# Strassen's seven products in an encoder block's gate and up projections, with the activations kept in DRAM and the merge's weights loaded once

## The chip, the cores and the metric

The kernel runs on one core of a Trainium2 chip. The metric is the device time of one execution in microseconds (us), the median of several runs. The engines are TensorE (PE in the profile; PEld is its weight load), VectorE (DVE), ScalarE (ACT), GpSimd (POOL) and SyncE (SP), whose queue issues every DMA of this kernel. SBUF is the memory on the chip, with 128 partitions; PSUM holds the results of matmuls; DRAM is the memory behind the DMAs.

## The reference

One encoder block over 1024 tokens and 16 learned ones ahead of them, in float32, width 1024. A mixer (retention and an attention with low-rank projections, merged by gates) and then a SwiGLU network of hidden width 2816:

```python
y_ret = (silu(rg) * y_ret) @ w_ret_out
y_mla = _mla_attention(q_nope, q_rope, k_nope, k_rope, v).reshape(B, L, 512) @ w_mla_out
merged = sigmoid(a_gret) * y_ret + sigmoid(a_gmla) * y_mla
h = h + merged @ w_o
u = _rmsnorm(h, norm_ffn_w)
h = h + (silu(u @ w_gate) * (u @ w_up)) @ w_down
return _rmsnorm(h, norm_final_w)[:, 16:]
```

## The kernel before

Everything is kept transposed: features on the partitions, the 1024 tokens along the free dimension, in two halves (c = 0, 1) of 512. A matrix product keeps float32 accuracy by splitting both operands x into a high part in the matmul's type (`hi`, a cast on ACT) and the rest (`lo = x - hi`, a subtraction on DVE). Each product of 128 features is then three matmuls, high by high, high by low and low by high (`mm3`, L117 to L119). Weights come from DRAM by `weights` (L109 the load, L112 the cast, L113 the low part), each as a block of 128 output features.

The order of the instructions on each engine is set by the Tile framework's scheduler, which works ahead as far as the buffers of a pool go. A tile's pool and its count of buffers so decide how early its load or split can stand.

The change lies in the last third of the program:

- Attention, 8 heads by 4 query chunks (`units`). It writes its output to DRAM (`o_d`) for the first six heads and to SBUF (`o3`) for the last two. The gates' and retention's results lie in DRAM as `s_d` and `r_d`.
- Load of `o_d` and its split (L803, L804) at the end of attention.
- Merge: for c, for m (8 blocks of 128 features): w_mo's block, four products of 128 features, times `s_d` (DVE, L825), plus `r_d` (POOL, L826), and a split (L812, L813). The block's weights are loaded for each c, 16 loads.
- w_o: for c, for m: weights, eight products of 128 features, plus x (L855) gives the residual `h2`, which stays in SBUF; times the norm's weights and split (ACT L857, DVE L858) into `u2`; squares on ACT, summed on POOL (L865, `ssum`). At the end of each c the norm's factor per token (`rs2_b`, L838 to L148).
- Gate and up: the 22 blocks of 128 hidden features are worked in groups of 6, 6, 6 and 4 (`FG`). For each block and each c, gate and up take 24 matmuls each; then `rs2_b` times gate (L891), Silu on ACT (L892), `rs2_b` times up (L893), their product on POOL (L894), and its split (L896, L897) into `hid`.
- Down: after each group, for 8 blocks m, the group's share of the down projection is added to `h2` (L919). In the last group the second half of the tokens is done in two chunks of 256, and the last norm and the stores (`finish`, L872, L875) follow.

```python
def gemm_s(ps, w, xs, kt, c, cols=slice(0, 512)):
    wh, wl = w
    for k in range(kt):
        ks = slice(k * P, (k + 1) * P)
        xh, xl = xs[k][c]
        mm3(ps, wh[:, ks], wl[:, ks], xh[:, cols], xl[:, cols], k == 0, k == kt - 1)
```

Of the kernel before, what the change touches and what calls it, by code (L numbers as in the profile page):

```python
# [35 lines left out]
FG = ((0, 6), (6, 6), (12, 6), (18, 4))  # L36

# [5 lines left out]
def build(nc, tc, A, out):  # L43
# [57 lines left out]
    l_d = mk(dram, (H, NB, P), "l_d")  # L101

# [18 lines left out]
    def gemm(ps, w, xs, kt, lo, n):  # L121
        wh, wl = w
        for k in range(kt):
            ks = slice(k * P, (k + 1) * P)
            xh, xl = xs[k]
            mm3(ps, wh[:, ks], wl[:, ks], xh[:, lo : lo + n], xl[:, lo : lo + n], k == 0, k == kt - 1)

# [446 lines left out]
    with ExitStack() as c1:  # L574
# [100 lines left out]
        def mix_values(hh, qc, pt, lb):  # L675
# [11 lines left out]
            if hh < H - 2:  # L687
                pool.tensor_mul(ta, ta, lb)
                store(o_d[hh // 2, hs, c], ta)
            else:  # L690
                pool.tensor_mul(o3[hs, c], ta, lb)
# [34 lines left out]
        wnext, late = None, None  # L726
# [6 lines left out]
        for i, (hh, qc) in enumerate(units):  # L733
# [3 lines left out]
            if hh % 2 == 1 and p < 3:  # L737
# [7 lines left out]
                elif qc == 2:  # L745
                    heads_q(p + 1, wnext[0], *QCH[1])
                    heads_q(p + 1, wnext[0], *QCH[2])
                    if p == 2:
                        right.close()
                        wp3 = sb(right2, "w3", 3, side="right")  # L750
                        wr3 = sb(right2, "w3r", 2, side="right")
                        t3 = sb(right2, "t3", 2, side="right")
                        t3b = sb(right2, "t3b", 3, side="right")
                        o3p = sb(right2, "o3", 1, side="right")
                        o3 = mk(o3p, (P, S), "o3")
# [14 lines left out]
    with ExitStack() as c1:  # L770
        wp = wp3
        hp = sb(c1, "h2")
        h2 = mk(hp, (P, KT, S), "h2")
        pm = sb(c1, "ps_mm3", 6, space=PSUM)
        pr_ = sb(c1, "ps_r3", 2, space=PSUM)
        r2c = mk(hp, (P, 32), "r2c")[:, :NB]
        rs2_b = mk(hp, (P, S), "rs2_b")
        slot_a = sb(c1, "slot_a", 16)
        slot = sb(c1, "slot", 40)
        ssum = [mk(hp, (P, 512), f"ssum{c}") for c in range(2)]  # L780

        def slots(pl=None):
            return mk(pl or slot, (P, 512), "slot", F32R), mk(pl or slot, (P, 512), "slot", F32R)

        def gemm_s(ps, w, xs, kt, c, cols=slice(0, 512)):
            wh, wl = w
            for k in range(kt):
                ks = slice(k * P, (k + 1) * P)
# [3 lines left out]
        o = []  # L792
        for k in range(4):
            oc = []
            for c in range(2):
                cs = slice(c * 512, c * 512 + 512)
                if k < 3:
                    raw = mk(t3, (P, 512), "ta3")
                    load(raw, o_d[k, :, cs])
                else:  # L800
                    raw = o3[:, cs]
                oh, ol = slots(slot_a)
                act.copy(oh, raw)  # L803
                dve.tensor_sub(ol, raw, f(oh))  # L804
                oc.append((oh, ol))
            o.append(oc)
        mg = [[None, None] for _ in range(KT)]
        held = None

        def split_merged(m, c, r):  # L810
            gh, gl = slots()
            act.copy(gh, r)  # L812
            dve.tensor_sub(gl, r, f(gh))  # L813
            mg[m][c] = (gh, gl)

        for c in range(2):
            cs = slice(c * 512, c * 512 + 512)
            for m in range(KT):
                w = weights(wp, A["w_mo"][m], 512, "w", wr3)
                sg, r = mk(t3b, (P, 512), "tb3"), mk(t3b, (P, 512), "tc3")  # L820
# [3 lines left out]
                gemm_s(ps, w, o, 4, c)  # L824
                dve.tensor_mul(sg, ps, sg)  # L825
                pool.tensor_add(r, r, sg)  # L826
                if held:
                    split_merged(*held)
                held = (m, c, r)
        split_merged(*held)  # L830
# [15 lines left out]
        u2 = [[None, None] for _ in range(KT)]  # L846
        for c in range(2):
            for m in range(KT):
                w = weights(wp, A["w_o"][m], D, "w", wr3)
                xk = mk(t3, (P, 512), "ta3")  # L850
                load(xk, A["xT"][m, :, c * 512 : c * 512 + 512])
                ps = mk(pm, (P, 512), "mm")
                gemm_s(ps, w, mg, KT, c)
# [152 lines left out]
```

## Time and profile before

| | |
|---|---|
| median of 3 runs | 1885.93 us (1884.98 to 1886.2) |
| profiled execution | 1885.32 us, span 1883.3 us |
| mean granted TensorE clock | 0.996 |
| TensorE busy | 1857.2 us, 99% |
| DVE, ACT, POOL busy | 880.3, 686.9, 351.4 us |
| DMA | 131.43 MB, 70 GB/s |
| merge begins | 1010.5 us |
| w_o, second half ends | about 1152 us |
| last matmul of the down projection | 1870.85 us |

A row of groups gives a line, engine, operation, tiles (out<-in), shapes, the count, the busy time, the mean of one in ns, and the idle time of the engine before them with what ended it. The chain is the sequence of work that ended last, followed back from the last instruction. In a timeline the first number is the start, the second the length, and the bracket tells how long the engine had been idle. A matmul's shown length (0.39 us) is longer than its share, since matmuls are pipelined; the distance from one to the next is what counts.

### The profile page before, as it was taken

The numbers are of one execution on the slowest core, as the hardware profiler recorded it, in microseconds if no ns is written. First come the engines' busy times: TensorE is split into PE (matmuls) and PEld (weight loads), VectorE is DVE, ScalarE is ACT, GpSimd is POOL, SyncE is SP. The second block draws the span as 40 slices with busy tenths as digits, with TensorE's granted clock in tenths as the row PEclk, the third lists the DMA queues.
The fourth block names the chain that finished last, engine by engine and source line by source line (L and its number), as shares of the span: only waits on it lengthen the run. The fifth ranks groups of instructions, "written<-read, shape, count | busy, mean of one in ns | idle before, by whom it ended". The sixth has DMA issues, their size and how long they took to land.

```text
span 1883.3 us, 24884 instructions
## 1 busy us (share of the span) xinstructions
PE 1857.2 (99%) x9806; PEld 1593.2 (85%) x9806; DVE 880.3 (47%) x1764; ACT 686.9 (36%) x1212; POOL 351.4 (19%) x324
## 2 busy tenths in 40 slices
PE   8999999999999999999999999999999999999997
PEld 8898989888888988999897788888888888888887
DVE  6654545452222436888787743223232223322335
ACT  6723233334111335877785443211122112211225
POOL 5303021204000012433423322110011001110111
PEclk9999999999999999999999999999999999999999
DMA  6101111124221213111213742111111111112112
GB/s 209 45 35 57 45 46 51 51 90 157 89 68 60 74 30 129 34 39 29 72 42 130 228 141 83 46 37 54 50 52 48 42 56 45 44 49 65 39 40 90
DMA packets 56197, 131.43 MB, mean 70 GB/s; under 512 B 7744, under 2 KB 16512, under 8 KB 56080
## 3 DMA queue, kind: packets, MB, share of 16 engines
q1 hardware_dynamic: 56080, 129.84, 21.7%
q8 instruction: 77, 1.26, 0.3%
q14 instruction: 40, 0.33, 0.1%
HBM read 108.87 MB, written 20.88 MB: 69 GB/s over the span
## 4 chain that ended last, share of the span: by engine, by line
PE 92%; DVE 3%; ACT 2%; DMA 2%; issue 1%; SPq 0%; POOL 0%; DVEq 0%; ACTq 0%; POOLq 0%
PE mm L117 24%; PE mm L119 24%; PE mm L118 24%; PE o L679 3%; PE t L649 3%; PE s L117 1%; PE s L119 1%; PE s L118 1%; PE tr L374 1%; DMA wr<-in_w_mo 1%; PE y L381 1%; PE u L362 1%; PE y L380 1%; DVE wl L113 1%; PE tr L395 1%
## 5 line engine op out<-in xcount | busy, mean ns | idle before, releaser
L119 PE MATMUL mm<-slot,wl 128*128 128x512 f32 (+1 forms) x1220 | 473.1, 388 | 0.6 <-DVE wl L113 0.5
L117 PE MATMUL mm<-slot,wh 128*128 128x512 f32 (+1 forms) x1220 | 471.6, 387 | 0.7 <-ACT wh L112 0.7
L118 PE MATMUL mm<-slot,wh 128*128 128x512 f32 (+1 forms) x1220 | 471.6, 387 | 0.0
L112 ACT CAST wh<-wr 128x1024 fp32r<-128x1024 f32 (+2 forms) x154 | 148.3, 965 | 514.6 <-PE mm L118 415.9
L119 PEld LDWEIGHTS mm<-slot,wl 128*128 128x128 f32 x1220 | 229.1, 188 | 50.6 <-DVE wl L113 4.6
L117 PEld LDWEIGHTS mm<-slot,wh 128*128 128x128 f32 x1220 | 229.1, 188 | 47.6 <-ACT wh L112 1.1
L118 PEld LDWEIGHTS mm<-slot,wh 128*128 128x128 f32 x1220 | 229.1, 188 | 46.8
L117 PE MATMUL mm<-uh,wh 128*128 128x512 f32 (+2 forms) x640 | 242.7, 379 | 1.0 <-DVE rk L317 0.6
L118 PE MATMUL mm<-ul,wh 128*128 128x512 f32 (+2 forms) x640 | 243.5, 380 | 0.0
L119 PE MATMUL mm<-uh,wl 128*128 128x512 f32 (+2 forms) x640 | 242.3, 379 | 0.0
L113 DVE TENSOR_TENSOR wl<-wr,wh 128x1024 fp32r<-128x1024 f32 (+2 forms) x154 | 189.1, 1230 | 37.2 <-ACT wh L112 35.3
L894 POOL TENSOR_TENSOR tb<-tb,ta 128x512 f32<-128x512 f32 x44 | 71.8, 1631 | 603.2 <-DVE tb L893 478.5
L117 PEld LDWEIGHTS mm<-uh,wh 128*128 128x128 f32 x640 | 120.3, 188 | 23.7 <-DVE rk L317 1.0
L119 PEld LDWEIGHTS mm<-uh,wl 128*128 128x128 f32 x640 | 120.5, 188 | 21.0
L118 PEld LDWEIGHTS mm<-ul,wh 128*128 128x128 f32 x640 | 120.2, 188 | 20.8
L893 DVE TENSOR_TENSOR tb<-mm,rs_b 128x512 f32<-128x512 f32 x44 | 30.4, 692 | 174.2 <-PE mm L119 174.1
L919 DVE TENSOR_TENSOR h<-mm,h 128x512 f32<-128x512 f32 (+1 forms) x72 | 45.2, 630 | 133.8 <-PE mm L119 133.7
L639 DVE TENSOR_SCALAR_CACHE_REDUCE pr<-s,sq_c 128x384 f32<-128x384 f32 (+1 forms) x192 | 103.0, 574 | 8.4 <-PE t L657 5.6
L652 DVE TENSOR_TENSOR ptl<-t,pth 128x512 fp32r<-128x512 f32 x128 | 85.8, 685 | 19.5 <-ACT pth L651 18.8
L896 ACT CAST slot<-tb 128x512 fp32r<-128x512 f32 x44 | 27.3, 621 | 180.3 <-POOL tb L894 180.3
L651 ACT CAST pth<-t 128x512 fp32r<-128x512 f32 x128 | 71.7, 580 | 26.6 <-PE t L649 26.2
L641 ACT ACTIVATE pr<-pr,nm 128x1040 f32<-128x1040 f32 x64 | 74.5, 1165 | 10.7 <-DVE nm L640 10.0
(324 smaller groups left out, 2993.9 us busy)
## 6 DMA issues: line engine op xcount, KB each, us to landing
wr<-in_w_in SPq DMA_DIRECT2D x37, 512.0 KB
wr<-in_w_g SPq DMA_DIRECT2D x22, 512.0 KB
wr<-in_w_u SPq DMA_DIRECT2D x22, 512.0 KB
wr<-in_w_d SPq DMA_DIRECT2D x24, 384.0 KB
wr<-in_w_o SPq DMA_DIRECT2D x16, 512.0 KB
z_d<-ay SPq DMA_DIRECT2D x16, 256.0 KB
s_d<-g SPq DMA_DIRECT2D x16, 256.0 KB
wr<-in_w_ro SPq DMA_DIRECT2D x8, 512.0 KB
```

Of the source, the lines that this page charges most:

```text
L112: act.copy(hi, raw)
L113: dve.tensor_sub(lo, raw, f(hi))
L117: pe.matmul(ps, sh, mh, start=start, stop=False)
L118: pe.matmul(ps, sh, ml, start=False, stop=False)
L119: pe.matmul(ps, sl, mh, start=False, stop=stop)
L639: dve.tensor_scalar(pr[:, c], ps[:, :n], sq_c[:, qb : qb + 1], None, ALU.mult, ALU.max, accum_out=mx[:, j : j + 1])
L641: act.activation(pr, pr, AF.Exp, bias=nm, accum_out=sums[:, s : s + 1])
L649: pe.transpose(tp[:, i, :], pr[:, b * P : (b + 1) * P], ident)
L651: act.copy(pt[0][d], tp)
L652: dve.tensor_sub(pt[1][d], tp, f(pt[0])[d])
L679: pe.matmul(po[:, :256], vt[:, b, hh, :], pt[j][:, b, :], start=(b == 0 and j == 0), stop=False)
L894: pool.tensor_mul(tu, tu, tg)
```

## The change

It does five things.

1. Gate and up are computed for blocks of 256 hidden features (11 of them) with Strassen's algorithm in Winograd's form on 2 x 2 blocks: the weights' four quarters are 256 x 256 pieces of (input half, output half), where an input half is every other block m of 128; the operand's four quarters are (input half, token half). `seven` loads four weight quarters, builds four sums of them on POOL (L905 to L908), makes seven products (`prod`, L923, 12 matmuls each, of which two add into a bank that holds an earlier product), and combines them with five additions on ACT and DVE (L933 to L942).
2. The operand's sums (`tb7`: "11", "21", "n1", "t2", "t3", "22", "t4") are made in w_o's second half from `hm` and `h0`, seven pairs of high and low tiles for each of four pairs of m. In the first gate seven (`late`) the first four products are done for three of the four pairs of m first, and then for the last pair.
3. The gated activations go to DRAM (`f_d`, L963) and come back for the down projection (L984), which stands after all 11 blocks; the residual goes to DRAM as `h_d` (L867) and is added in the first down group.
4. The merge runs over m outside and c inside, so w_mo's blocks are loaded and split 8 times in place of 16. The s_d and r_d tiles come from a pool `hr` of ten tiles that lies where the attention's memory was. All weights behind the merge come in pieces of 512 columns (`pieces`).
5. The `o_d` loads and their splits stand in attention units (6, 1) to (7, 2). The last stores leave one block at a time.

```diff
+O_AT = ((6, 1), (6, 2), (6, 3), (7, 0), (7, 1), (7, 2))
...
+    h_d = mk(dram, (KT, 2, P, 512), "h_d")
+    f_d = mk(dram, (22, 2, P, 512), "f_d")
...
+    def split(t, ph, plo):
+        hi, lo = slot(ph, F32R), slot(plo, F32R)
+        act.copy(hi, t)
+        dve.tensor_sub(lo, t, f(hi))
+        return hi, lo
...
+                        wr3 = sb(right2, "w3r", 5, side="right")
+                        wh3 = sb(right2, "w3h", 4, side="right")
+                        wl3 = sb(right2, "w3l", 4, side="right")
+                        xr = sb(right2, "x3", 14, side="right")
...
+            if (hh, qc) in O_AT:
+                g = O_AT.index((hh, qc))
+                raw = slot(wr3)
+                load(raw, o_d[g // 2, :, (g % 2) * 512 : (g % 2) * 512 + 512])
+                o_s.append(split(raw, xr, xr))
...
+        bt = sb(c1, "blocks", 58)
+        hr = sb(c1, "h3", 10)
+        ws3 = sb(c1, "w3s", 4)
+        pm = sb(c1, "ps_mm3", 7, space=PSUM)
...
-        for c in range(2):
-            cs = slice(c * 512, c * 512 + 512)
-            for m in range(KT):
-                w = weights(wp, A["w_mo"][m], 512, "w", wr3)
+        for m in range(KT):
+            w = pieces(A["w_mo"][m], 512)
+            for c in range(2):
...
-                hm = h2[:, m, c * 512 : c * 512 + 512]
+                hm = slot(hr)
                 dve.tensor_add(hm, ps, xk)
+                store(h_d[m, c], hm)
+                wc = column(C_FFN + m)
+                t7 = tb7[m // 2]
+                if c == 0:
+                    h0[m] = hm
+                    hi, lw = slot(bt, F32R), slot(bt, F32R)
+                    act.mul(hi, hm, wc)
+                    dve.scalar_tensor_tensor(lw, hm, wc, f(hi), ALU.mult, ALU.subtract)
+                    t7["11" if m % 2 == 0 else "21"] = (hi, lw)
+                elif m % 2 == 0:
+                    g12, n1 = slot(xr), slot(xr)
+                    act.mul(g12, hm, wc)
+                    dve.scalar_tensor_tensor(n1, h0[m], wc, g12, ALU.mult, ALU.subtract)
+                    t7["n1"] = split(n1, bt, bt)
+                else:
+                    g22, t2 = slot(xr), slot(xr)
+                    act.mul(g22, hm, wc)
+                    dve.tensor_add(t2, g22, n1)
+                    t7["t2"] = split(t2, bt, bt)
+                    pool.tensor_sub(g12, g22, g12)
+                    t7["t3"] = split(g12, bt, bt)
+                    t7["22"] = split(g22, bt, bt)
+                    dve.scalar_tensor_tensor(t2, h0[m], wc, t2, ALU.mult, ALU.subtract)
+                    t7["t4"] = split(t2, bt, bt)
...
+        def seven(src, pl, post, late=False):
+            a11, a21, a22, a12 = [slot(wr3) for _ in range(4)]
+            for i, t in enumerate((a11, a21, a22, a12)):
+                load(t, src[i])
+            s1, s2, s3, s4 = [slot(ws3) for _ in range(4)]
+            pool.tensor_add(s1, a21, a22)
+            pool.tensor_sub(s2, s1, a11)
+            pool.tensor_sub(s3, a11, a21)
+            pool.tensor_sub(s4, s2, a12)
...
+            todo = (("a", a11, "11"), ("b", s2, "t2"), ("c", s3, "t3"), ("d", s1, "n1"))
+            if late:
+                for t in todo:
+                    prod(*t, range(3))
+            tail = range(3, 4) if late else range(4)
+            e, v = slot(pl), slot(pl)
+            act.copy(e, prod(*todo[0], tail))
+            dve.tensor_add(e, prod(*todo[1], tail), e)
+            dve.tensor_add(v, prod(*todo[2], tail), e)
+            dve.tensor_sub(v, v, prod(*todo[3], tail))
+            post("22", v)
+            post("11", prod("a", a12, "21"))
+            t = slot(pl)
+            dve.tensor_add(t, prod("c", a22, "t4"), e)
+            post("21", t)
+            dve.tensor_sub(e, e, prod("d", s4, "22"))
+            post("12", e)
...
+            def gate_post(name, t):
+                cs = slice(0, 512) if name[1] == "1" else slice(512, 1024)
+                if name == "11":
+                    g = slot(xr)
+                    dve.tensor_mul(g, t, rs2_b[:, cs])
+                else:
+                    g = t
+                    pool.tensor_mul(g, g, rs2_b[:, cs])
+                act.activation(g, g, AF.Silu)
+                pool.tensor_mul(g, g, rs2_b[:, cs])
+                sil[name] = g
+            def up_post(name, t):
+                g = sil[name]
+                dve.tensor_mul(g, t, g)
+                store(f_d[2 * j + int(name[0]) - 1, int(name[1]) - 1], g)
...
+                    raw = slot(xr)
+                    load(raw, f_d[j, c])
+                    hc.append(split(raw, bt, bt))
...
+                if gi == 0:
+                    raw = slot(hr)
+                    load(raw, h_d[m, c])
+                    acc[m][c] = slot(bt)
+                    dve.tensor_add(acc[m][c], ps, raw)
+                    continue
```

How rows move on three engines is shown next. Tiles of the new code are all called slot; L138 is the low part of `split`, L809 that of `pieces`.

DVE in the middle of the merge, before: three rows to a step, the weight's low part (L113), the product with s_d (L825), and the low part of the merged tile (L813).

```order
L113 TENSOR_TENSOR wl_10370<-wr_10367,wh_10369 128x512
L825 TENSOR_TENSOR tb_1868_10315<-mm_10319,tb_1868_10315 128x512
L813 TENSOR_TENSOR slot_10335<-tc_1861_10287,slot_10334 128x512
L113 TENSOR_TENSOR wl_10399<-wr_10396,wh_10398 128x512
L825 TENSOR_TENSOR tb_1876_10344<-mm_10348,tb_1876_10344 128x512
L813 TENSOR_TENSOR slot_10364<-tc_1869_10316,slot_10363 128x512
```

DVE in the same place, now:

```order
L809 TENSOR_TENSOR slot_10429<-slot_10426,slot_10428 128x512
L138 TENSOR_TENSOR slot_10244<-slot_10196,slot_10243 128x512
L138 TENSOR_TENSOR slot_10267<-slot_10225,slot_10266 128x512
L834 TENSOR_TENSOR slot_10276<-mm_10280,slot_10276 128x512
L138 TENSOR_TENSOR slot_10296<-slot_10248,slot_10295 128x512
L834 TENSOR_TENSOR slot_10299<-mm_10303,slot_10299 128x512
```

The weight's low part stands once for two steps.

DVE at the end of w_o's second half, before: for each m the residual (L855), a weight's low part (L113) and the operand's low part (L858).

```order
L855 TENSOR_TENSOR h_1800_10107<-mm_11223,ta_2070_11221 128x512
L113 TENSOR_TENSOR wl_11319<-wr_11316,wh_11318 128x1024
L858 SCALAR_TENSOR_TENSOR slot_11250<-h_1800_10107,cols_74,slot_11249 128x512
L855 TENSOR_TENSOR h_1800_10107<-mm_11264,ta_2078_11262 128x512
L113 TENSOR_TENSOR wl_11445<-wr_11442,wh_11444 128x1024
L858 SCALAR_TENSOR_TENSOR slot_11291<-h_1800_10107,cols_74,slot_11290 128x512
```

DVE in the same place, now, from the last residual (L866) on: t2 (L884) and its low part, t4 (L889), the low parts of t3, "22" and t4, and between them those of two weight pieces for the first gate seven (slot_11539 and slot_11573 as high parts).

```order
L866 TENSOR_TENSOR slot_11439<-mm_11414,slot_11412 128x512
L138 TENSOR_TENSOR slot_11540<-slot_11488,slot_11539 128x512
L884 TENSOR_TENSOR slot_11443<-slot_11442,slot_11390 128x512
L138 TENSOR_TENSOR slot_11447<-slot_11443,slot_11446 128x512
L889 SCALAR_TENSOR_TENSOR slot_11443<-slot_10966,cols_74,slot_11443 128x512
L138 TENSOR_TENSOR slot_11452<-slot_11389,slot_11451 128x512
L138 TENSOR_TENSOR slot_11456<-slot_11442,slot_11455 128x512
L138 TENSOR_TENSOR slot_11461<-slot_11443,slot_11460 128x512
L138 TENSOR_TENSOR slot_11574<-slot_11483,slot_11573 128x512
L934 TENSOR_TENSOR slot_11552<-mm_11510,slot_11552 128x512
```

Where one low part followed the last residual, five operand rows and two weight rows do, ahead of the first sum of products (L934).

POOL from the end of w_o on, before: the last sums of squares and then one product for each hidden tile.

```order
L865 TENSOR_TENSOR ssum_1804_10123<-ssum_1804_10123,tc_2074_11253 128x512
L865 TENSOR_TENSOR ssum_1804_10123<-ssum_1804_10123,tc_2082_11294 128x512
L894 TENSOR_TENSOR tb_2094_11373<-tb_2094_11373,ta_2093_11372 128x512
L894 TENSOR_TENSOR tb_2100_11433<-tb_2100_11433,ta_2099_11432 128x512
L894 TENSOR_TENSOR tb_2112_11505<-tb_2112_11505,ta_2111_11504 128x512
```

POOL in the same place, now:

```order
L906 TENSOR_TENSOR slot_11643<-slot_11642,slot_11634 128x512
L907 TENSOR_TENSOR slot_11644<-slot_11634,slot_11635 128x512
L886 TENSOR_TENSOR slot_11389<-slot_11442,slot_11389 128x512
L896 TENSOR_TENSOR ssum_1824_10146<-ssum_1824_10146,slot_11464 128x512
L908 TENSOR_TENSOR slot_11645<-slot_11643,slot_11637 128x512
L905 TENSOR_TENSOR slot_11791<-slot_11784,slot_11785 128x512
L957 TENSOR_TENSOR slot_11589<-slot_11589,rs_b_10144 128x512
L955 TENSOR_TENSOR slot_11553<-slot_11553,rs_b_10144 128x512
L955 TENSOR_TENSOR slot_11593<-slot_11593,rs_b_10144 128x512
L906 TENSOR_TENSOR slot_11792<-slot_11791,slot_11783 128x512
```

The first two rows are sums for the first up seven; they stand ahead of the last t3 (L886) and the last sum of squares (L896). The sums of the second gate seven (slot_11791, slot_11792) stand among the first seven's gate products (L955, L957).

More of the change, by code (lines that the diff above doesn't have):

```diff
@@ L724, in build @@
         ptp = sb(c1, "pt", 2)
-        wnext, late = None, None
+        wnext, late, o_s = None, None, []
         def mix(what):
@@ L770, in build @@
     with ExitStack() as c1:
[L771 to L783, printed above, removed]
@@ L785, in gemm_s, with wsplit @@
-        def gemm_s(ps, w, xs, kt, c, cols=slice(0, 512)):
-            wh, wl = w
+        kp = sb(c1, "keep")
+        r2c = mk(kp, (P, 32), "r2c")[:, :NB]
+        rs2_b = mk(kp, (P, S), "rs2_b")
+        ssum = [mk(kp, (P, 512), f"ssum{c}") for c in range(2)]
+        bt = sb(c1, "blocks", 58)
+        hr = sb(c1, "h3", 10)
+        ws3 = sb(c1, "w3s", 4)
+        pm = sb(c1, "ps_mm3", 7, space=PSUM)
+        pr_ = sb(c1, "ps_r3", 1, space=PSUM)
+        def wsplit(t):
+            return split(t, wh3, wl3)
@@ new lines, in pieces, with gemm_p @@
+        def pieces(src, n):
+            w = []
+            for lo in range(0, n, 512):
+                c = min(512, n - lo)
+                raw = slot(wr3)
+                load(raw[:, :c], src[:, lo : lo + c])
+                hi, low = slot(wh3, F32R), slot(wl3, F32R)
+                act.copy(hi[:, :c], raw[:, :c])
+                dve.tensor_sub(low[:, :c], raw[:, :c], f(hi)[:, :c])
+                w.append((hi, low))
+            return w
+        def gemm_p(ps, w, xs, kt, c, cols=slice(0, 512)):
@@ L795, in build @@
+        held = None
+        for m in range(KT):
+            w = pieces(A["w_mo"][m], 512)
             for c in range(2):
                 cs = slice(c * 512, c * 512 + 512)
[L797 to L814, printed above, removed]
-        for c in range(2):
-            cs = slice(c * 512, c * 512 + 512)
-            for m in range(KT):
-                w = weights(wp, A["w_mo"][m], 512, "w", wr3)
-                sg, r = mk(t3b, (P, 512), "tb3"), mk(t3b, (P, 512), "tc3")
+                sg, r = slot(hr), slot(hr)
@@ L862, in build @@
                 else:
-                    t = mk(t3b, (P, 512), "tc3")
+                    t = slot(xr)
                     act.square(t, hm)
@@ new lines, in build @@
+        for j in range(11):
+            sil = {}
+            def gate_post(name, t):
[13 more added lines that the diff above has]
+                store(f_d[2 * j + int(name[0]) - 1, int(name[1]) - 1], g)
+            seven(A["w_g"][j], xr, gate_post, j == 0)
+            seven(A["w_u"][j], hr, up_post)
@@ L877, in build @@
         prev = None
+        acc = [[None, None] for _ in range(KT)]
         for gi, (g0, gn) in enumerate(FG):
```

102 lines of the change are left out of this document (49 added, 53 removed).

## The prediction

> **What bounds the kernel now.** I read the head of the page first: engine shares, slices, granted clock, chain.
>
> ```profile
> span 1883.3 us, 24884 instructions
> ...
> PE 1857.2 (99%) x9806; PEld 1593.2 (85%) x9806; DVE 880.3 (47%) x1764; ACT 686.9 (36%) x1212; POOL 351.4 (19%) x324
> ...
> PE   8999999999999999999999999999999999999997
> ...
> PEclk9999999999999999999999999999999999999999
> ...
> PE 92%; DVE 3%; ACT 2%; DMA 2%; issue 1%; SPq 0%; POOL 0%; DVEq 0%; ACTq 0%; POOLq 0%
> ```
>
> TensorE is busy in every slice at a full clock and is 92% of the chain. Time can come only from fewer matmuls or from the few places where it idles. Next the busy time by stretch (span, engines, granted clock, DMA share, GB/s): attention, merge, w_o, then gate, up and down.
>
> ```profile
> core 0: us, PE busy (x) PEld busy (x) DVE busy (x) ACT busy (x) POOL busy (x), PEclk, DMA share, GB/s
> 900.00:1000.00 100.00, 96.77 (x699) 90.81 (x698) 82.68 (x254) 77.74 (x170) 32.01 (x49) 1.00 0.18 53
> 1010.40:1062.00 51.60, 50.26 (x210) 38.30 (x210) 38.83 (x48) 20.71 (x34) 24.88 (x17) 1.00 0.70 231
> 1066.00:1152.00 86.00, 86.00 (x389) 71.45 (x388) 41.30 (x49) 38.12 (x52) 25.06 (x14) 1.00 0.48 146
> 1200.00:1400.00 200.00, 200.00 (x884) 165.62 (x883) 59.57 (x73) 34.13 (x44) 19.94 (x12) 1.00 0.16 48
> ```
>
> From 1200 to 1400 there is nothing but 512-wide matmuls without a gap: 200/884 = 0.2262 us each. The merge's 210 should last 47.5 us and take 51.6, so it loses 4.1. The waits say to what (the first three rows from 1003 to 1062, the last TensorE's own after 1062; total, times, longest):
>
> ```profile
> POOL tc L826 <- DVE tb L825: 19.8, 11, 4.7
> ...
> ACT wh L112 <- DMA wr<-in_w_mo: 6.5, 7, 1.5
> ...
> PEld mm L119 <- DVE wl L113: 4.6, 12, 1.0
> ```
> ```profile
> PE r L145 <- DVE r2c L843: 1.2, 1, 1.2
> ```
>
> TensorE waits for the low half of the weight, which stands behind the load of w_mo. Behind the merge it waits only in the last norm. The later stages are TensorE's own time, and every cover there is large.
>
> **The two vector engines.** All that the change adds falls to DVE and POOL. Prices (count, busy us, mean ns):
>
> ```profile
> L897 DVE TENSOR_TENSOR slot<-tb,slot 128x512 fp32r<-128x512 f32 x44 | 30.4, 691 | 78.3 <-ACT slot L896 78.3
> L893 DVE TENSOR_TENSOR tb<-mm,rs_b 128x512 f32<-128x512 f32 x44 | 30.4, 692 | 174.2 <-PE mm L119 174.1
> L858 DVE SCALAR_TENSOR_TENSOR slot<-h,cols,slot 128x512 fp32r<-128x512 f32 x16 | 11.9, 747 | 0.0
> L894 POOL TENSOR_TENSOR tb<-tb,ta 128x512 f32<-128x512 f32 x44 | 71.8, 1631 | 603.2 <-DVE tb L893 478.5 <-ACT wh L112 124.7
> L896 ACT CAST slot<-tb 128x512 fp32r<-128x512 f32 x44 | 27.3, 621 | 180.3 <-POOL tb L894 180.3
> L892 ACT ACTIVATE ta<-ta 128x512 f32<-128x512 f32 x44 | 27.8, 632 | 68.5 <-DVE ta L891 68.5
> ```
>
> Why L894 has a mean of 1.63 the timeline shows (start, length):
>
> ```profile
> 1171.77 1.29 POOL L894 TENSOR_TENSOR tb<-tb,ta 128x512 f32<-128x512 f32 x1 [10.53 <-DVE tb L893]
> 1182.66 1.28 POOL L894 TENSOR_TENSOR tb<-tb,ta 128x512 f32<-128x512 f32 x1 [9.60 <-DVE tb L893]
> 1193.56 2.37 POOL L894 TENSOR_TENSOR tb<-tb,ta 128x512 f32<-128x512 f32 x1 [9.62 <-ACT wh L112]
> ```
> ```profile
> 1171.84 2.30 DVE L113 TENSOR_TENSOR wl<-wr,wh 128x1024 fp32r<-128x1024 f32 x1 [0.21 <-ACT wh L112]
> ...
> 1188.12 1.23 DVE L113 TENSOR_TENSOR wl<-wr,wh 128x1024 fp32r<-128x1024 f32 x1 [0.17 <-ACT wh L112]
> ...
> 1193.56 1.23 DVE L113 TENSOR_TENSOR wl<-wr,wh 128x1024 fp32r<-128x1024 f32 x1 [0.17 <-ACT wh L112]
> ```
>
> Alone, POOL's operation takes 1.28 and DVE's 1.23. Where both run, whichever started second is longer by nearly all of the other (2.37; 2.30). They take turns. L893, which reads PSUM and one tile in SBUF, has no such rows: its mean over 44 is 0.692. So I add DVE operations with two SBUF inputs and POOL's into one "exclusive" sum and leave DVE's readings of PSUM out.
>
> [...]
>
> **Gate and up.** Now 22 weight blocks x 2 token halves x 2 projections x 24 = 2112 matmuls; then 11 x 2 x 7 products x 12 = 1848. The 264 removed are worth 264 x 0.2262 = **-59.7 us** if the rest keeps its pace. In a pair of sevens (gate and up of one j) TensorE has 168 x 0.2262 = 38.0 us. In that time:
> - DVE: 14 low halves and 3 products in SBUF, 17 x 0.691 = 11.7 exclusive; 12 readings of PSUM, 8.3.
> - POOL: 8 weight sums and 7 gate products, 15 x 1.28 = 19.2.
> - ACT: 14 casts, 2 copies, 4 Silu, about 16 x 0.621 + 4 x 0.632 = 12.5.
> - DMA: 8 loads and 4 stores of 256 KB, 3.1 MB: 83 GB/s beside the merge's 231.
>
> Exclusive: 31.0 of 38.0; with all of DVE in series, 39.3. POOL's order has the sums of a seven before the gate products of the seven ahead of it, so their lead is most of a seven (19 us). SP's loads stand behind f_d stores that wait for the up products, but a seven ahead too. I cost this at nothing; the cover is the 7 us per pair, and when it is gone the low half of a weight is late at TensorE. Bounds: 0 to 11 x (39.3 - 38.0) = 14 us.
>
> **The operands (w_o, c = 1).** For each pair of m TensorE has 48 x 0.2262 = 10.9 us. Exclusive on DVE: two L879/L889 forms 1.49, t2's sum 0.69, five low halves 3.46, four of weights 2.76: 8.4. On POOL: t3 and two sums of squares, 3.8. Together 12.2 for 10.9. Before, the same stretch had DVE at 41.3 and POOL at 25.1 of 86. Four pairs need 49 us; ahead of the last t3 in the queues stand also the low halves of the first four products (2.8) and seven weight sums on POOL (9.0), and behind it some 3.4: 57 us. They begin with the first hm, 5.4 us into c = 1: ready at 5.4 + 57 = 62, of which splits done ahead take off 2.8: 60. TensorE, which takes three quarters of the first four products before it needs the last pair, arrives at 43.4 + 43 x 0.2262 = 53.1. I take **+7**; 0 if the lock binds less, 12 if DVE's eight PSUM sums (5.5) come in series too.
>
> **The merge.** Per step DVE and POOL had L813 0.69, L113 0.69 and L826 1.28 exclusive, 2.66 of TensorE's 2.71 us; now the weight's low half comes every second step: 2.32. DMA falls from 768 to 640 KB per step. But the s_d and r_d tiles now lie where attention's memory was, so none is loaded before its end; seven PSUM banks (19 us) cover that. Of the 4.1 us I take **-3.5** (0 to -4.1).
>
> **Attention's end.** The chain there:
>
> ```profile
> 1001.78 1.10 DVE slot L804
> ...
> 1002.90 2.53 DMA ta<-o_d
> ...
> 1006.10 0.37 ACT oa L682
> ...
> 1010.49 0.43 PE mm L117
> ```
>
> ACT stood at the o_d load and the last units' copies stood behind it; TensorE went on without a gap at 1010.49. Six loads and splits move into earlier units, where ACT has 22% free and DVE 17%. **-1**, from -2 to +3 (the 3.2 us that TensorE already idles there, doubled).
>
> **DRAM trips and the end.** 60 stores and 60 loads of 256 KB, 31 MB, spread over 700 us. In the last seven (19.0 us) DVE splits 12 activations beside 16 operations of its own: 28 x 0.691 = 19.3. The first down product needs the last of them only 3 us after it begins. **+1.5**; 0 if covered, 12 x (0.691 + 0.621) = 15.7 if none is. In the down groups nothing else changes but the h_d loads, covered by 36 matmuls each. The end:
>
> ```profile
> 1873.35 6.25 SPq L875 DMA_DIRECT2D out_y<-h  x4
> ...
> 1876.23 0.86 DVEq L1001
> 1877.10 2.06 DVE h L872 x3
> ```
>
> The last stores leave one by one, 128 KB instead of 512: **-0.5** (-1 to +1).
>
> **Sum**, against the profiled execution (1885.3; its span 1883.3 and 2.0 around it): -59.7 - 3.5 - 1 + 7 + 1.5 - 0.5 = -56.2, so 1829.1. The median of the runs is 0.6 above this execution: 1829.7, said as 1830.
>
> **Rivals.**
> 1. The operand stage is covered: the 36 matmuls of the four late products absorb all, and only the 0 to 1.5 elsewhere remains: 1822. For it: DVE's sum without the lock is 8.4 + 1.4 of 10.9 a pair. Against: 2.37 for 1.28.
> 2. The lock binds in every pair, as in-order queues let exclusive work bunch: +14, 1844. Against: 18% of the pair is free.
> 3. The activations' way back through DRAM holds the first down group: the 12 splits come after the last seven, +14, 1844. Against: their loads have over a hundred us of room, except slots that free only as the last seven uses its operands.
> 4. Slower than before: a seven's second product waits each time for the chain POOL sum, POOL sum, cast, low half. Locked, that is 2 x 2.37 + 0.62 + 1.97 = 7.3, less the first product's 2.7: 4.6 us x 22 = 101, 1931. It decides from 56/22 = 2.6 us per seven. For it: every sum is now ahead of a product on the slowest engine. Against: the order puts sums a seven ahead.
> That the products aren't saved is excluded: TensorE's order is 264 rows shorter.
>
> **How the numbers follow.** Forecast 0.56 (own range 1823 to 1838); rival 1 0.16; rival 2 0.14; rival 3 0.09; rival 4 0.05, of which 0.01 would stay within 0.2%. A difference under 0.2% (3.8 us) can't be told from no change here. Faster by more 0.95, the same 0.01, slower 0.04. The range reaches from the covered case with attention's better bound (1818) to the two +14 cases with a little of a second one: 1850.
>
> **What would show it.** Right: TensorE 264 matmuls fewer; from 1250 on nine tenths and a pair each 38.0 us; a wait of TensorE on L138 of 5 to 10 us near the first seven, with POOL's L886 and L896 stretched beyond 1.28; the merge's 192 in about 44 us. Wrong: gaps inside later sevens, with L138 (DVE) or L905 to L908 (POOL) as releaser; f_d or h_d loads as releaser at the first down product; L138 at a mean near 0.7 beside POOL, which would mean that they don't take turns.

## The result and the profile after

The changed kernel takes 1825.84 us (median of 4 runs, 1825.05 to 1827.8), beside 1885.97 for the kernel before (4 runs). The ratio is 0.9684, with a 95% interval from 0.9667 to 0.97: 60 us faster, where 56 were forecast. A second series of the changed kernel gave 1827.38 (1824.69 to 1830.21), so a difference of one or two microseconds between two kernels below is not told apart by the times alone; for those the stretches of the profiles are compared.

The head of the page after, with the row of the new products:

```profile
span 1823.6 us, 25696 instructions
...
PE 1796.3 (99%) x9542; PEld 1543.0 (85%) x9542; DVE 1018.3 (56%) x2007; ACT 753.5 (41%) x1394; POOL 528.1 (29%) x449
...
PE 89%; DVE 4%; ACT 2%; issue 2%; POOL 1%; DMA 1%; SPq 0%; DVEq 0%; ACTq 0%; POOLq 0%
...
L923 PE MATMUL mm<-slot,slot 128*128 128x512 f32 x1848 | 422.0, 390 | 2.4 <-DVE slot L138 2.2
```

TensorE has 264 instructions fewer and is still 99% busy. DVE, ACT and POOL have more work, and none of it shows in the chain except a few per cent. The new products (the row of L923) had to wait 2.4 us in all, in 22 sevens.

The stretches that answer to those shown of before: the merge with the first w_o products, the first gate seven (26.06 us), one of the 20 in the middle (19.04), one pair, and the whole steady part up to the second down group.

```profile
core 0: us, PE busy (x) PEld busy (x) DVE busy (x) ACT busy (x) POOL busy (x), PEclk, DMA share, GB/s
1008.70:1060.00 51.30, 51.30 (x227) 42.48 (x227) 35.64 (x45) 17.71 (x31) 25.60 (x18) 1.00 0.67 222
...
1160.00:1630.00 470.00, 470.00 (x2080) 389.28 (x2079) 257.84 (x357) 143.53 (x243) 235.21 (x158) 1.00 0.31 103
```
```profile
1141.30:1167.36 26.06, 23.37 (x102) 18.45 (x100) 23.26 (x29) 13.36 (x23) 14.46 (x9) 0.93 0.26 80
1167.36:1186.40 19.04, 19.04 (x86) 15.77 (x84) 14.16 (x15) 6.33 (x12) 15.02 (x12) 1.00 0.26 83
```
```profile
1224.48:1262.56 38.08, 38.08 (x170) 31.53 (x168) 20.80 (x29) 12.01 (x21) 22.38 (x16) 1.00 0.25 83
```

The merge, which had 210 matmuls in 51.6 us, now has 227 in 51.3: no loss. From 1160 to 1630 TensorE never stops. In a pair (38.08 us) DVE shows 20.80 and POOL 22.38, where 20.0 and 19.2 were forecast; POOL's 15 operations would take 19.2 us at 1.28 each; I read the excess as time in which it stood behind DVE. The one place that lost time is the first gate seven, 26.06 for 19.04, with a granted clock of 0.93. TensorE's waits from the merge on (total, times, longest) name it:

```profile
PE mm L923 <- DVE slot L138: 2.2, 1, 2.2
PE r L158 <- DVE r2c L852: 1.2, 1, 1.2
PE mm L121 <- ACT slot L137: 0.8, 1, 0.8
...
PE r L847 <- POOL ssum L896: 0.3, 1, 0.3
```

The wait of 2.2 is for the low half of a weight sum (s3). The 0.3 is for the last sum of squares, and the experiments show that this small one is the one that counts. The 1.2 belongs to the last norm, as before the change, and the 0.8 lies between the first two down groups. The groups of DVE and POOL from 1104 to 1158, where the operands are made, show the two engines holding each other up (the lock, as I call it; count, busy us, mean ns):

```profile
L138 DVE TENSOR_TENSOR slot<-slot,slot 128x512 fp32r<-128x512 f32 x25 | 22.5, 932 | 3.7 <-ACT slot L137 3.4
...
L896 POOL TENSOR_TENSOR ssum<-ssum,slot 128x512 f32<-128x512 f32 x7 | 11.6, 1663 | 10.6 <-ACT slot L895 10.6
...
L889 DVE SCALAR_TENSOR_TENSOR slot<-slot,cols,slot 128x512 f32<-128x512 f32 x4 | 4.9, 1231 | 0.0
...
L866 DVE TENSOR_TENSOR slot<-mm,slot 128x512 f32<-128x512 f32 x7 | 4.8, 683 | 1.9 <-PE mm L123 1.1 <-DMA slot<-in_xT 0.8
```

Operations with two SBUF inputs are stretched (0.93 for 0.69, 1.66 for 1.28, 1.23 for 0.75). L866, which reads PSUM, keeps its 0.68.

### The profile page after: what moved, and what is told of

It is laid out like the page before. It is cut to its first block, busy times and chain, and to the rows that moved or that the text cites. A ratio compares the mean times of both kernels' runs of the same rounds, so it can differ in the third digit from the quotient of the medians.

```text
span 1823.6 us, 25696 instructions
## 1 busy us (share of the span) xinstructions
PE 1796.3 (99%) x9542; PEld 1543.0 (85%) x9542; DVE 1018.3 (56%) x2007; ACT 753.5 (41%) x1394; POOL 528.1 (29%) x449
## 3 DMA queue, kind: packets, MB, share of 16 engines
q8 instruction: 75, 1.23, 0.3%
## 4 chain that ended last, share of the span: by engine, by line
PE 89%; DVE 4%; ACT 2%; issue 2%; POOL 1%; DMA 1%; SPq 0%; DVEq 0%; ACTq 0%; POOLq 0%
PE mm L923 22%; PE mm L121 16%; PE mm L122 16%; PE mm L123 16%; PE o L692 3%; PE t L662 3%; PE s L121 1%; PE s L123 1%; PE s L122 1%; PE tr L387 1%; PE y L394 1%; PE u L375 1%; PE y L393 1%; DVE pr L652 1%; DVE ptl L665 1%
## 5 line engine op out<-in xcount | busy, mean ns | idle before, releaser
L923 PE MATMUL mm<-slot,slot 128*128 128x512 f32 x1848 | 422.0, 390 | 2.4 <-DVE slot L138 2.2
L923 PEld LDWEIGHTS mm<-slot,slot 128*128 128x128 f32 x1848 | 347.7, 188 | 75.6 <-DVE slot L138 3.2
L137 ACT CAST slot<-slot 128x512 fp32r<-128x512 f32 x247 | 149.6, 621 | 263.7 <-PE mm L923 222.9
L138 DVE TENSOR_TENSOR slot<-slot,slot 128x512 fp32r<-128x512 f32 x247 | 207.8, 857 | 49.2 <-ACT slot L137 48.4
L122 PE MATMUL mm<-slot,slot 128*128 128x512 f32 (+1 forms) x576 | 217.2, 377 | 0.0
L123 PE MATMUL mm<-slot,slot 128*128 128x512 f32 (+1 forms) x576 | 217.1, 377 | 0.0
L121 PE MATMUL mm<-slot,slot 128*128 128x512 f32 (+1 forms) x576 | 216.0, 378 | 0.8 <-ACT slot L137 0.8
L808 ACT CAST slot<-slot 128x512 fp32r<-128x512 f32 x91 | 51.4, 564 | 184.0 <-PE mm L122 149.0
L121 PEld LDWEIGHTS mm<-slot,slot 128*128 128x128 f32 x576 | 108.3, 188 | 21.6 <-ACT slot L137 1.5
L123 PEld LDWEIGHTS mm<-slot,slot 128*128 128x128 f32 x576 | 108.4, 188 | 19.9
L122 PEld LDWEIGHTS mm<-slot,slot 128*128 128x128 f32 x576 | 108.4, 188 | 19.9
L116 ACT CAST wh<-wr 128x1024 fp32r<-128x1024 f32 x51 | 53.2, 1049 | 152.5 <-PE mm L122 120.5
L809 DVE TENSOR_TENSOR slot<-slot,slot 128x512 fp32r<-128x512 f32 x91 | 59.0, 648 | 58.6 <-ACT slot L808 56.1
L973 POOL TENSOR_TENSOR slot<-slot,rs_b 128x256 f32<-128x256 f32 (+1 forms) x9 | 9.3, 1063 | 255.0 <-ACT rs_b L161 255.0
```

The source lines that it names most:

```text
L116: act.copy(hi, raw)
L121: pe.matmul(ps, sh, mh, start=start, stop=False)
L122: pe.matmul(ps, sh, ml, start=False, stop=False)
L123: pe.matmul(ps, sl, mh, start=False, stop=stop)
L137: act.copy(hi, t)
L138: dve.tensor_sub(lo, t, f(hi))
```

## The experiments

All start from the changed kernel. Times are medians of 4 runs; the stretches come from the profile of each run, by the starts of TensorE's matmuls in the timeline.

**1. The changed kernel once more.**

> The changed kernel once more, to see how much of a few us between two runs is chance. All theories: 1825 to 1828. The start of the merge stood at 1008.7 us in the first profile and between 1009.6 and 1011.2 in the four variants, whose code up to there is the same; if that is chance, it lies anywhere between here too, and the 1.7 us by which the merge starts earlier than before the change are no proven gain.

It took 1827.38 us. Its stretches equal those of the first profile, which stand second in each pair (merge 43.66 and 43.66 us, w_o 88.92 and 88.92, the 22 sevens 426.77 and 426.58, down 243.83 and 243.87). What differs is ahead of the merge: over all profiles of variants with the same code up to there the merge began between 1007.8 and 1011.8 us. Before the change it began at 1010.4. So the 1.7 us by which the first profile starts it earlier lie within chance, and no gain of the earlier o_d loads is shown.

**2. The merge with c outside again**, so that w_mo's blocks are loaded and split 16 times:

```diff
-        for m in range(KT):
-            w = pieces(A["w_mo"][m], 512)
-            for c in range(2):
+        for c in range(2):
+            for m in range(KT):
+                w = pieces(A["w_mo"][m], 512)
```

> The changed kernel with one part undone: the merge again runs over c outside and m inside, so w_mo's blocks are loaded and split 16 times, but with the five raw and four split buffers of the change. If the number of weight splits and loads set the merge's pace (2.66 us of exclusive DVE and POOL work for 2.71 us of TensorE), the merge lasts about 46 to 47 us again and the time is about 1829. If the merge before was held only by its two raw buffers (a load can't start before a buffer is free), five of them hide the loads, the merge keeps 43.7 us and the time is 1826.

The merge took 43.87 us beside 43.66. The time was 1828.78, but the difference of the spans, 2.9 us, lies in other stretches (1.2 of it ahead of the merge, 0.7 in w_o). Loading the weights twice costs the merge 0.2 us. That is the rival's result: my account by the exclusive sum (2.66 of 2.71 us a step) was not what slowed the merge before.

**3. The same with two raw buffers for w_mo**, used in turn as before the change:

```diff
+        raws = [slot(wr3) for _ in range(2)]
...
-                w = pieces(A["w_mo"][m], 512)
+                w = pieces(A["w_mo"][m], 512, raws[m % 2])
```

> As the run with c outside in the merge (w_mo loaded 16 times), but with two raw buffers for w_mo in turn, as before the change. If the merge before was paced by the rotation of two buffers, each taken for a load of 4.1 us, a cast of 0.64 and a subtraction of 0.70 (5.5 to 5.8 us for two steps, so 2.8 to 2.9 a step), the merge lasts 45.5 to 47 us again, 2 to 3 more than 43.9: about 1830. If the buffers don't matter, 43.9 as with five.

The time was 1831.43 us, and the merge took 45.79. The stretch of the merge with five buffers (the first row) and with two (the second), and what the casts waited for with two:

```profile
1009.90:1054.00 44.10, 44.10 (x194) 36.18 (x194) 37.47 (x40) 16.70 (x30) 22.76 (x15) 1.00 0.86 276
```
```profile
1007.80:1053.50 45.70, 45.43 (x193) 35.40 (x193) 33.30 (x40) 16.64 (x30) 22.06 (x15) 1.00 0.83 266
```
```profile
ACT slot L808 <- DMA slot<-in_w_mo: 12.2, 10, 3.0
```

TensorE is without a pause in the first and not in the second, and ACT waits for w_mo's loads again. The merge was paced by the turn of two raw buffers: two of them bring back 1.9 of the 3.2 us by which it was longer before the change (46.83), whichever loop is outside. Most of the rest is a wait of w_o's first product for its own weights. The profile before has two such waits, of which the first falls into the merge's 46.83:

```profile
1057.25 0.50 PE L117 MATMUL mm<-slot,wh 128*128 128x512 f32 x1 [0.71 <-ACT wh L112]
...
1058.51 0.50 PE L119 MATMUL mm<-slot,wl 128*128 128x512 f32 x1 [0.53 <-DVE wl L113]
```

No run here takes these waits apart. DMA ran at 276 GB/s without harm.

**4. Without the four late products**, that is with the first gate seven like every other:

> The changed kernel, but in the first gate seven the first four products aren't split into three quarters and a last one. If the last pair's operands set the wait there, TensorE needs t2 of the last pair after 21 matmuls in place of 39, so the wait grows by up to 18 x 0.227 = 4 us: about 1830. If the wait is that of the weight sum's low half (s3, held up in DVE's queue), it is needed later now (after 24 matmuls in place of 18), and the operands come at about the same time: 1825 to 1827.

1828.44 us; the first gate seven took 27.37 us beside 26.06 and 26.25. It lies between the two theories: the splitting of the first four products is worth some 1.2 us at most here, not 4, and TensorE's waits were 2.7 us for DVE and 1.6 for ACT. Even the 1.2 is not clear of chance: in experiment 3, whose code in this stage is that of the changed kernel, the first gate seven took 27.15.

**5. Without POOL's seven sums of squares for the second token half**, whose norm this kernel therefore leaves incomplete:

```diff
-                    pool.tensor_add(ssum[c], ssum[c], t)
+                    if c == 0:
+                        pool.tensor_add(ssum[c], ssum[c], t)
```

> The changed kernel without the seven additions on POOL that sum the squares of the second token half (that half's norm is then wrong). They take 7 x 1.66 us on POOL while the operands are made. If DVE and POOL lock each other out and this sets the wait in the first gate seven (2.4 us and 1.6 us at a lower clock, some 5 us with the small ones), it falls to 0 to 1.5: 1821 to 1823. If the wait is the chain of dependent operations behind the last w_o product on DVE and ACT alone, nothing changes: 1826.

1823.58 us, and the first gate seven fell from 26.06 to 21.46. The only wait of TensorE left there is the norm's own:

```profile
PE r L158 <- DVE r2c L852: 1.1, 1, 1.1
```
```profile
1143.02:1164.48 21.46, 20.36 (x95) 16.67 (x95) 18.77 (x26) 13.74 (x24) 12.32 (x8) 1.00 0.27 87
```

So 4.6 us of the loss hang on POOL's seven additions. The run takes away two things at once, their own time in POOL's queue and the time for which they hold DVE and DVE holds them (1.66 us each for 1.28 in the rows above), and doesn't say how much each is worth. The clock is whole again too.

**6. Work for TensorE in the wait**: 12 matmuls whose result nobody uses, ahead of the third product of the first gate seven.

```diff
+                        with tc.issue_after(last[0].ins):
+                            for i in range(12):
+                                pe.matmul(fill, tb7[0]["11"][0][:, :P], tb7[0]["11"][1], start=i == 0, stop=i == 11)
```

> The changed kernel with 12 matmuls of 128x512, whose result nobody uses, ahead of the third product of the first gate seven, where TensorE waits 2.4 us (12 x 0.227 = 2.7 us). If the lower clock that follows there (0.43 us a matmul for 3.4 us) comes from the idle time before it, it vanishes: -1.6 us, +0.3 for the surplus, and one copy on ACT: the 22 sevens take 425.3 in place of 426.6, the time is 1824 to 1826. If the lower clock has another cause, the slow matmuls stay: 1826 to 1828.

Neither came out: 1832.74 us, and the first gate seven took 32.65. The wait for s3 was filled (the 0.3 us for DVE that is left stands earlier, at the second product) and the clock stayed at 1.00 there. But then TensorE met the next wait:

```profile
PE r L847 <- POOL ssum L896: 4.3, 1, 4.3
```
```profile
1155.26 1.71 POOL L896 TENSOR_TENSOR ssum<-ssum,slot 128x512 f32<-128x512 f32 x1
```
```profile
1146.00:1152.00 6.00, 6.00 (x28) 4.77 (x27) 6.00 (x7) 2.31 (x4) 4.08 (x4) 1.00 0.06 22
1157.00:1159.00 2.00, 1.98 (x9) 1.98 (x10) 1.72 (x3) 0.54 (x2) 0.00 (x0) 0.50 0.03 8
1159.00:1165.00 6.00, 6.00 (x15) 4.65 (x16) 1.97 (x4) 2.23 (x5) 0.00 (x0) 0.51 0.05 17
```

POOL ends its last sum at 1157.0, and the norm's product with it stands in TensorE's order before the rest of the seven. In the changed kernel the same sum ends at 1156.1 (it begins at 1154.33), and TensorE comes there at the same moment, since it has already lost its time at s3 and to the low clock. What sets this stage is the end of POOL's queue; the wait for s3 and the slow matmuls before it lie in its shadow.

The 4.3 us are more than the changed kernel would show: with the filling matmuls in it, the order of TensorE has the norm's product after 31 matmuls of the seven in place of 43. The 12 that now stand behind it (2.7 us) could have run in the wait; by that estimate 1.6 us of it would be left. The low clock came here too, during the 4.3 us and until 1164.9, and with the 12 matmuls it about makes up the 32.65.

The other profiles with this stage's code bear the shadow out. POOL's last sum of squares there, in the changed kernel and in experiment 3:

```profile
1154.33 1.73 POOL L896 TENSOR_TENSOR ssum<-ssum,slot 128x512 f32<-128x512 f32 x1
```
```profile
1157.30 1.72 POOL L897 TENSOR_TENSOR ssum<-ssum,slot 128x512 f32<-128x512 f32 x1
```

It ends 14.77, 14.93, 15.15 and 15.83 us after the first gate seven begins (first and second series, experiments 2 and 3), and the seven takes 26.06, 26.25, 26.47 and 27.15: 11.3 us more each time. The first three had the low clock behind the wait for s3 and the last had not, so that low clock cost nothing.

**7. Three of the squares summed by TensorE**, with one-column products in the norm:

> The changed kernel, but the last three squares of the second token half aren't added on POOL; TensorE adds them in its product with ones (12 matmuls of one column each, about 1.4 us). If the lock between DVE and POOL sets the wait, three POOL operations fewer (5 us) take most of the 5 us away: 1822 to 1824. If not: 1827, slower by the 12 matmuls.

1828.1 us, the first gate seven 28.07: no gain. The wait for DVE was gone (1.2 us for one of the squares on ACT remained), but the norm now has 24 one-column matmuls in 2.5 us. They keep TensorE busy, and half the clock follows them as it follows idle time:

```profile
1150.90:1153.40 2.50, 2.50 (x24) 2.50 (x23) 1.78 (x3) 0.62 (x1) 2.50 (x2) 0.98 0.09 30
1153.40:1160.20 6.80, 6.80 (x19) 5.54 (x20) 3.38 (x6) 2.70 (x6) 0.63 (x1) 0.51 0.12 39
```

6.8 us at half clock, about half of them lost.

**8. All of them summed by TensorE in full-width products** of a 128 x 128 tile of ones, which gives the sum on every partition at once:

```diff
+                if c == 1:
+                    if m == 0:
+                        sums = mk(pr_, (P, 512), "r3")
+                    t = slot(xr, F32R)
+                    act.square(t, hm)
+                    pe.matmul(sums, ones_r, t, start=m == 0, stop=m == KT - 1)
...
+        act.activation(rs2_b[:, 512:], sums, AF.Sqrt, bias=eps_c, scale=1.0 / D)
+        dve.reciprocal(rs2_b[:, 512:], rs2_b[:, 512:])
```

> A version that may be faster. The second token half's squares are summed over the features by TensorE: a product of ones (128 x 128) with each of the eight tiles, into one PSUM bank, which gives the sum on every partition at once; the root and the reciprocal then work on 128 x 512. It removes seven POOL additions and the norm's one-column products while the operands are made, and adds 8 x 0.227 = 1.8 us on TensorE and one DVE reciprocal of 128 x 512, which no trace shows. If the lock sets the wait in the first gate seven: -4.6 + 1.8 - 0.7 = -3.5, 1822. If the reciprocal is long (over some 4 us) it holds DVE's queue and gives the gain back: 1826.

1826.54 us (1823.97 to 1826.74); ratio to before 0.9683 (0.9668 to 0.9697), beside 0.969 (0.9676 to 0.9705) of the changed kernel on the same chip. In the profile w_o and the sevens together take 513.2 us in place of 515.5, so about 2 us are gained, which the times can't confirm. The reciprocal is the price that no trace had shown, between the two cases of the expectation:

```profile
L908 DVE RECIPROCAL rs_b<-rs_b 128x512 f32<-128x512 f32 x1 | 3.3, 3346 | 0.0
```

**9. POOL's weight sums for the first up seven queued behind the last sum of squares.**

```diff
+            if behind:
+                with tc.issue_after(last_sum.ins):
+                    sums(True)
```

> A version that may be faster. POOL's four sums for the first up seven, and the fourth for the first gate seven, are queued behind the last sum of squares, so four POOL operations (4 x 1.66 us) fewer stand among the making of the operands. If the lock of DVE and POOL sets the wait, it falls by most of 4.6 us, as where seven sums were left out, and the lower clock behind it goes too: the 22 sevens take 422 to 423.5, the time is 1822 to 1824. If it is DVE's own queue, 426.6 and 1826 to 1827 stay.

It was slower: 1830.51 us, the first gate seven 30.5. POOL's last sum of squares was ready at 1153.2, 3 us earlier, but now the fifth product had to wait:

```profile
PE mm L937 <- DVE slot L138: 3.8, 2, 2.5
PE r L847 <- POOL ssum L896: 1.1, 1, 1.1
```

```profile
1160.59 4.63 PE L937 MATMUL mm<-slot,slot 128*128 128x512 f32 x10 [2.53 <-DVE slot L138]
```

Fifty matmuls of the seven stand ahead of this row. It begins with the first one that needs the low half of a12, which is no weight sum. DVE makes it last of three low halves, and beside them POOL runs the sums that were put behind:

```profile
1155.39 5.14 DVE L138 TENSOR_TENSOR slot<-slot,slot 128x512 fp32r<-128x512 f32 x3
```
```profile
1154.88 1.75 POOL L907 TENSOR_TENSOR slot<-slot,slot 128x512 f32<-128x512 f32 x1
1156.71 1.61 POOL L908 TENSOR_TENSOR slot<-slot,slot 128x512 f32<-128x512 f32 x1
1158.28 1.71 POOL L909 TENSOR_TENSOR slot<-slot,slot 128x512 f32<-128x512 f32 x1
```

Three low halves of 0.69 each take 5.14 us. So the sums that were moved out of POOL's way to the norm held DVE instead: this order moved the wait from one engine's queue to the other's. A version with fewer sums behind was not tried.

**10. More POOL work in the sevens.** Four operations more in each of 20 sevens, as additions of two SBUF tiles, as memsets of the same tile, and two additions:

```diff
             pool.tensor_sub(s4, s2, a12)
+            for _ in range(4 if extra else 0):
+                pool.tensor_sub(ssum[0], ssum[1], ssum[0])
```

> The changed kernel with four more POOL operations in each of 20 sevens (j > 0), additions of two SBUF tiles whose result nobody uses. If DVE operations with two SBUF inputs and POOL's exclude each other, the exclusive sum of a pair of sevens grows from 31.0 to 31.0 + 8 x 1.28 = 41.2 us and passes TensorE's 38.1: 3.1 us a pair are lost, +31, about 1857. If the engines only share time now and then, POOL has 19.2 + 10.2 = 29.4 and DVE 20 of 38.1, and nothing is lost: 1826.

> As the run with four more additions, but the four operations on POOL only write (a memset of the same tile). If the lock is between two readers of SBUF, as the rows with 2.37 us for 1.28 let one think, DVE goes on beside a memset and nothing is lost whatever the memset takes up to 2.3 us: 1826. If any POOL operation holds up DVE, some 8 times the memset's length are added to 31.0 a pair: 1826 for up to 0.9 us, 1857 for 1.28.

> As the run with four more POOL additions in each of 20 sevens, but with two. The exclusive sum of a pair is 31.0 + 4 x 1.28 = 36.1 us against TensorE's 38.1, so nothing is lost if the sum is all that counts: 1826 to 1828. If queues in fixed order lose time well below the full sum, some of the 2 us of room is already gone: 1830 to 1840.

The times were 1860.09, 1826.81 and 1842.79 us. The first two came near their number, the third missed; but all three ran otherwise than written, so that the nearness of the first is in part luck. Nothing holds the extra operations, so POOL's queue took them early: the two additions per seven stand in the first three pairs (one of the 40 in the fourth), the four in the first six; the memsets, which have less to wait for, stand in w_o's second half and in the first two pairs. A pair's row tells how many there were. First the third pair with two additions (32 POOL operations) and the fifth (16, none left), then the fourth with four (30), then the second with memsets (37):

```profile
1235.54:1282.34 46.80, 40.85 (x170) 32.39 (x169) 29.95 (x30) 11.36 (x21) 46.41 (x32) 0.96 0.21 68
1320.41:1358.49 38.08, 38.08 (x169) 31.53 (x168) 20.80 (x29) 12.01 (x21) 22.37 (x16) 1.00 0.27 84
```
```profile
1324.47:1367.09 42.62, 40.43 (x170) 32.47 (x168) 28.54 (x28) 11.47 (x21) 42.15 (x30) 0.96 0.22 66
```
```profile
1185.77:1223.85 38.08, 38.08 (x170) 31.54 (x168) 23.56 (x29) 11.67 (x21) 34.24 (x37) 1.00 0.24 84
```
```profile
L910 POOL MEMSET ssum<- 128x512 f32 x47 | 24.7, 526 | 1.8
```

From the second pair on, a pair with extra additions has 28 to 31 of POOL's and DVE's 17. Its sum of exclusive work is 28 x 1.28 + 11.7 = 47.5 to 51.4 us, and those pairs took 41.2 to 46.8 in place of 38.1: POOL is busy, or locked, all of the pair (46.41 of 46.80), and TensorE waits. So the engines do exclude each other, and POOL and DVE do become the bound. The sum overstates by 3 to 6 us a pair. In part that can be the small overlap of two operations that meet: in the rows of the prediction, 1.28 and 1.23 took 2.37 together, 0.14 less than their sum, which would make 4 us if each of 28 additions met one (an estimate). Pairs with 15 to 18 POOL operations lose nothing; none with 19 to 27 was measured. As memsets of 0.53 us, 47 in two pairs and 20 of them in the pair shown, POOL's extra work cost nothing at all. The memsets' busy time alone would not have filled a pair, but their 10.5 us with the 31.0 would have, had they locked DVE out.

## Why the prediction was right, and where it wasn't

| term | forecast | measured (profile to profile) |
|---|---|---|
| 264 products fewer | -59.7 | -59.8: 84 matmuls in 19.04 us, 264 x 0.2267 |
| merge, with w_o's first products | -3.5 | -4.1 (merge 46.83 to 43.66, w_o 89.85 to 88.92) |
| attention's end | -1 | -1.7, within chance |
| operands, first gate seven | +7 | about +5 (26.06 less 19.04, less 1.6 of the norm's products, as before); 4.6 of it hang on POOL's seven additions |
| seven to down, down groups | +1.5 | +1.3 |
| the end | -0.5 | -0.6 (12.49 to 11.88), within chance (12.24 in the second series) |
| span | -56.2 | -59.7 |

The stretches go by the starts of TensorE's matmuls; by these, w_o's second half ended before the change at 1147.1 us, and not at about 1152 as in the table ahead of the prediction.

The largest term came out as written because the steady part kept TensorE's pace: the sum of exclusive work in a pair, 31.0 of 38.1, was below the bound, and experiment 10 shows that it was indeed the right sum to form, since with twice the POOL additions the pair was no longer TensorE's. POOL operations that only write did not count in it: the run with memsets had 37 POOL operations in a pair, which took 38.08 us as without them. Rival 2, the lock in every pair, is thereby out for this kernel: the runs show a loss with 28 POOL operations in a pair and none with 18. Rivals 3 and 4 are out as well, since TensorE never stopped from 1160 to 1630, through the later sevens and into the first down group. Rival 1, no loss at the operands, is out by the 4.6 us of experiment 5.

The operand stage had the right mechanism as far as the runs show it (the rows there are stretched, and in experiment 9 DVE takes 5.14 us for what takes 2.07 alone; how much of the loss is the lock and how much POOL's own work stays open), and two wrong details. Its size was 7 and is about 5. Its place was put at the last pair's t3, which TensorE needs after 43 matmuls. The first wait came earlier, at the low half of s3 after 20, because DVE's queue holds it behind the operands of the third pair and the first of the fourth; and the last came at the norm's product with POOL's sum of squares, which I had left behind t3's end in my sum. Experiment 6 shows that the second is the one that binds. The sign that the prediction gave for this stage, a wait of 5 to 10 us on L138, was not seen: it is 2.2, and the loss is spread over this wait, the slow matmuls behind it and the norm.

The merge term had nearly the right size by the wrong step, which is luck. I put the loss before to the exclusive work of DVE and POOL and the gain to half the weight splits. Experiments 2 and 3 show that neither mattered much: with five raw buffers the merge with twice the splits is as fast (43.87), and with two it is slow again (45.79). Another 0.9 of the term lies in w_o (89.85 to 88.92). Both waits of its first product, shown with experiment 3, stood in the 51.6 us that I read as the merge's. The row I quoted, ACT waiting for w_mo's load, already said so; I read it as a matter of how many loads there are, and it was one of how early a load can start.

The seven-to-down term hit its size at another place. TensorE went from the last seven to the first down group without a wait, and lost 1.3 us between the first and the second group, where 12 casts and splits of activations stand behind the last weights of the group. I had said that nothing else changes there. That the size fits is luck too.

## What to carry to other kernels

When DVE and POOL share a stage, add the operations of DVE with two SBUF inputs and those of POOL that read SBUF into one sum and compare it with the bound of the stage, stage by stage: here 31 of 38 cost nothing, and where it was 12.2 of 10.9 some 5 us were lost. Before work is taken out of a stage that waits for loads, look at how many buffers the load turns through; more raw buffers gave most of what half the loads were thought to give. And a wait that is seen can lie in the shadow of a later one: filling it tells which of them binds.

## What was not expected of the hardware

After the wait of 2.2 us TensorE was granted half its clock for 3.4 us, somewhat later:

```profile
1146.30:1148.70 2.40, 0.17 (x2) 0.03 (x1) 2.40 (x4) 1.14 (x2) 1.17 (x1) 1.00 0.00 0
1150.00:1153.40 3.40, 3.40 (x10) 2.66 (x9) 2.68 (x4) 1.72 (x3) 2.77 (x3) 0.52 0.21 77
```

Matmuls stood 0.43 us apart in place of 0.227. The profiles of the first and the second series and of experiment 2 have it; those of experiments 3 and 4 have the same wait and kept 1.00. Experiment 7 had it for 6.8 us after a row of one-column matmuls with no idle time just before it, and experiment 6 until 1164.9, some 8 us of matmuls, after 4.3 of idle time. Beside the lengths of 3.4 and 6.8 us the starts show the same step: within each trace the spells of half clock begin whole multiples of 3.413 us apart. In the first profile they begin at 692.46, 1149.84 and 1815.44 us, which is 134 and then 195 times 3.4133.

The windows of 3.413 us that these starts mark also tell how much idle time stood ahead of a spell. Cut so, the first profile has its wait inside one window, and the next one has half the clock. In experiment 3, with nearly the same wait (2.25 us), a border falls into it, counted back from the spell at 1820.14 of its own trace:

```profile
1146.43:1149.84 3.41, 1.18 (x6) 0.98 (x6) 3.41 (x5) 1.08 (x2) 2.12 (x2) 1.00 0.00 0
1149.84:1153.25 3.41, 3.41 (x10) 2.63 (x9) 2.69 (x3) 1.86 (x3) 2.78 (x3) 0.50 0.21 77
```
```profile
1147.71:1151.13 3.42, 1.68 (x8) 1.04 (x6) 3.42 (x3) 1.14 (x2) 2.73 (x2) 1.00 0.09 32
1151.13:1154.54 3.41, 2.90 (x12) 2.12 (x13) 3.36 (x5) 1.26 (x3) 2.19 (x2) 1.00 0.20 77
```

TensorE is without work for 2.23 of 3.41 us in the first profile's window, and for 1.73 and 0.51 in the two of experiment 3. The same holds over all traces from 1010 to 1810 us, if the norm's narrow products are counted as no work. Of the 15 spells that begin there, 14 follow a window with 1.99 us or more without work, and one (in the run with four additions) a window with 1.71; none of some 3,200 other windows at full clock has more than 1.85 (in the first profile none has more than 0.87). So in these runs half the clock came after a window that was without work for about half of its 3.413 us (1.71 at the least) or more, and two profiles with the same wait differ in where the border falls. What ends a spell after one window or after several was not worked out.
